# mLSTM output with tokens on the partitions: divisor from two columns of ones beside v

## The chip, the cores and the metric

The kernel runs on one core of a Trainium2 chip, in one launch. The metric is the device time in microseconds (us). Three runs of the kernel before took 1508.81 to 1511.1 us, median 1509.54.

## The reference, cut to what matters

The model is two transformer blocks on 256 tokens of width 1024. The change is in the token mixer of the first block, in the mLSTM (8 heads, 64 wide in q and k, 128 wide in v). The reference walks over chunks of 64 tokens; the kernel computes the same thing for all 256 tokens at once, as masked attention with gate weights. Per head h and token t:

```python
# w[s,t] = (q_t . k_s) * exp(gate terms - m_t), for s <= t, else 0
num[t,:] = sum_s w[s,t] * v[s,:]
den[t]   = sum_s w[s,t]
h[t,:]   = num[t,:] / maximum(abs(den[t]), exp(-m_t))     # exp(-m_t) is "floor" below
hm = h * rsqrt(mean(h*h, axis=-1) + EPS)                  # over the 128 channels of the head
ym = sigmoid(o) * (hm * mh_norm_w)                        # o: one of the projections
```

With D = max(|den|, floor) the division and the norm are one factor: hm = num * rsqrt(sum(num*num)/128 + EPS*D*D). Both kernels use that form, and sigmoid(o) as (1 + tanh(o/2))/2.

## The kernel before, in words

Activations lie with features on the partitions: [128, 8, 256] is 8 tiles of 128 features by 256 tokens. A projection of 128 output features is one `gemm` (L180): 24 matmuls of 256 columns on TensorE, three for each of 8 slices (high half of the weight by high half of the input L185, high by low L186, low by high L187). The weights arrive by DMA (queue of SP, 1 MB each) into three buffers; ScalarE makes the rounded half `wh` (L165) and VectorE or GpSimd the rest `wl` (L166), ahead of the gemm, into a ring of four buffers; a buffer comes free when the gemm that read it is done.

The part around the change, in order:

- L550 to L666: q, k, v and the gates. `wide` makes v with tokens on the partitions, and L209 copies it out of PSUM. `gates` (L612) makes the running sums, the floor (L637, [40, 256], heads on partitions) and the column form `acol` of the gate term (two small transposes, L642, copied at L643).
- L678 `head(h)`: five stages, one taken at each call of `advance`. Scores sc (L681, L682), gate row spread over the partitions (L600), three VectorE operations and an exp for the weights (L686 to L692), the product w (L694), the matmuls num (L697, L698: stationary v, moving w, result features by tokens) and den (L699, L700: stationary `eh(h)`, 40 columns of which two are ones, so that row h of one PSUM tile collects head h), the copy nso (L702), the square sq (L704) and its sum ssq (L705, stationary `eh(h)` again).
- L717: eight rounds of three gemms, with four stages of heads between the gemms of one round, and two slices of the ada projection (L425, VectorE, 32 slices in `adapt`) after each.
- L739: eight gemms for o; the heads left are finished after the first; L747 multiplies nso by 1 + tanh.
- L751 to L759: the factor for all heads as rows [40, 256]: |den|, max with the floor, square, scale, add ssq, root (L757), reciprocal (L758), and its two rounded halves hr.
- L762: eight gemms with tanh (tga). L778: eight more (tgm), and after each one head of `normed` (L769): row h of hr spread over the partitions by a matmul (L600, into the one PSUM tile `bc`), times nso and the norm weight (L773), split into ymh and yml (L262, L263). These feed the branch gemms from about 290 us on.

A planner places all of this: it simulates the engines and orders the instructions of each one by program order among those that are ready. Each engine then takes its own queue strictly in that order and waits where an input is late. All matmuls of `head` have f32 operands, which run as two passes each (the trace counts 16 records for 8 matmuls); those of `gemm` run as one. A transpose on TensorE runs as one.

Of the kernel before, what the change touches and what calls it, by code (L numbers as in the profile page):

```python
# [19 lines left out]
EPS = 1e-6  # L20
# [92 lines left out]
def body(ctx: ExitStack, tc: tile.TileContext, a: dict):  # L113
# [81 lines left out]
    def wide(ws, out, ps_tile, xh, xl, scale=None):  # L195

        ps = [ps_tile() for _ in range(2)]
        for i in range(2):
            wh, wl = next(ws)
            for t in range(2):  # L200
                ts_ = slice(t * 128, (t + 1) * 128)
                for k in range(4):
                    n, kk = slice(256 * k, 256 * k + 256), 4 * i + k
                    T.matmul(ps[t], lhsT=xh[:, kk, ts_], rhs=wh[:, n], start=kk == 0, stop=False)
                    T.matmul(ps[t], lhsT=xl[:, kk, ts_], rhs=wh[:, n], start=False, stop=False)
                    T.matmul(ps[t], lhsT=xh[:, kk, ts_], rhs=wl[:, n], start=False, stop=kk == 7)  # L206
        for t in range(2):
            if scale is None:
                A.copy(out(t), ps[t])  # L209
            else:  # L210
                A.activation(out(t), ps[t], AF.Copy, scale=scale[:, t:t + 1])

# [199 lines left out]
    with ExitStack() as p1:  # L412
# [4 lines left out]
        A.dma_start(out=col, in_=a["cols"])  # L417
        A.dma_start(out=cst["a"], in_=a["ca"])

        def big(name, slot, dt=F32):  # L420
            return f8.tile([128, 8, 256], dt, tag=f"s{slot}", name=name)

        def product(raw, j):
            scr = m1.tile([128, 1024], F32, tag="adas", name="scr", bufs=2)
            return V.scalar_tensor_tensor(out=scr, in0=raw, scalar=0.5, in1=crow, op0=ALU.mult, op1=ALU.mult,  # L425
                                          accum_out=ada[:, j:j + 1])

# [25 lines left out]
        def bct():  # L453
            return bank("bc", 256)
# [5 lines left out]

        def load_c():

            c1, t1 = (m1.tile([128, 1024], F32, tag="adas", name=n, bufs=2)[:1] for n in ("c1", "t1"))
            tc.keep_in_program_order(SY.dma_start(out=c1, in_=a["c"]))
            A.activation(t1, c1, AF.Tanh, scale=0.5)
            V.scalar_tensor_tensor(out=c1, in0=t1, scalar=1.0, in1=c1, op0=ALU.add, op1=ALU.mult)
            for n in range(F0):
                T.matmul(psb[:, :128], lhsT=ones, rhs=ones, start=True, stop=True)
            for i in range(2):
                early[:] = [T.matmul(banks[i], lhsT=ones[:1, :], rhs=c1[:, i * 512:(i + 1) * 512], start=True, stop=True)]  # L470
                A.copy(crow[:, i * 512:(i + 1) * 512], banks[i])
# [14 lines left out]
        def adaload(src, t, n):  # L486
            b = f"{t}{n & 6}"
            if n % 2 == 0:
                if where[b]:
                    stage[b] = f8.tile([128, 2048], F32, tag=f"s{where[b]}", name="araw")  # L490
                else:
                    stage[b] = m1.tile([128, 2048], F32, tag="araw", name="araw", bufs=2)
            raw = halfload(stage[b], src[n // 2], n % 2)
            warm(f"{t}{n}", raw)
            return raw
# [12 lines left out]
        def load_w(n):  # L508
            p = halfload(raws[n // 2], a["wqk"][n // 2], n % 2)
            warm(f"W{n}", p)  # L510
            if n < 4:
                ws.append(split(p, G if WG >> n & 1 else V))
                return
            t = f8.tile([128, 2048], F32R, tag=f"s{(4, 8)[n - 4]}", name="w4")
            with tc.issue_after(made[0].ins), tc.issue_after(made[1].ins):
                A.copy(t[:, :1024], p)
                (G if WG >> n & 1 else V).tensor_sub(t[:, 1024:], p, t[:, :1024].bitcast(F32))
            more.append((t[:, :1024], t[:, 1024:]))
# [72 lines left out]
                V.scalar_tensor_tensor(out=kk[:, j - 4, :], in0=t, scalar=1.0, in1=y, op0=ALU.add, op1=ALU.mult)  # L591

        floor = m1.tile([40, 256], F32, name="floor")
        negm, hr = (m1.tile([40, 256], F32R, name=n) for n in ("negm", "hr"))
        selr = m1.tile([40, 8], F32R, name="selr")

        def spread_row(row, h):
# [8 lines left out]
            A.copy(out, src)  # L606
            V.tensor_sub(out[at:], src[at:n], out[at:].bitcast(F32))

        acol = m1.tile([128, 2, 8], F32, name="acol")
        rw = m1.tile([128, 5, 256], F32, name="rw")  # L610

        def gates(wif):  # L612
# [27 lines left out]
            pt = bct()  # L640
            for t in range(2):
                T.transpose(pt[:, 8 * t:8 * t + 8], g[:8, 3, t * 128:(t + 1) * 128], C("ident")[:8, :8])  # L642
            V.tensor_copy(acol, pt[:, :16].rearrange("p (t h) -> p t h", t=2))  # L643


        v = big("v", 4)
        v4 = v.rearrange("p (t b) n -> p t b n", t=2)
        cv = chunks(a["wv"], range(4), pool_=PV)
        cst["b"] = m1.tile([128, NCST["b"]], F32, name="cb")
        for t in ORD2.split():  # L650
            n = int(t[1])
            if t[0] == "w":
                w67 = split(halfload(raw3, a["wqk"][3], n))
            elif t[0] == "l":
                wif = m1.tile([128, 8, 72], F32, name="wif")
                tc.keep_in_program_order(SY.dma_start(out=wif, in_=a["wif"].rearrange("p (k n) -> p k n", k=8)))
                SY.dma_start(out=cst["b"], in_=a["cb"])
            elif t[0] == "q":
                pss.append(mmt())
                gemm(pss[-1], w67, hh, hl)  # L660
            elif t[0] == "u":
                unit_qk(pss[n], n)
            elif t[0] == "v":
                wide(cv, lambda t: v4[:, t, n, :], mmt, hh, hl)
            elif t[0] == "g":
                gates(wif)  # L666
        vt = v.rearrange("p (t b) n -> p t (b n)", t=2)


        den = bank("den", 256)[:40]  # L670
        ssq = bank("ssq", 256)[:40]

        def eh(h):
            return C("eh")[:, 7 - h:47 - h]

        nso = big("nso", 5)

        def head(h):  # L678
            sc = bank("sc", 384)
# [3 lines left out]
            nb = spread_row(negm, h)  # L683
            yield
            w = m1.tile([128, 384], F32, tag="mw", name="mw", bufs=2)
            V.scalar_tensor_tensor(out=w[:, 0:128], in0=nb[:, 0:128], scalar=acol[:, 0, h:h + 1], in1=C("mneg"),  # L686
                                   op0=ALU.add, op1=ALU.add)
            V.scalar_tensor_tensor(out=w[:, 256:384], in0=nb[:, 128:256], scalar=acol[:, 1, h:h + 1], in1=C("mneg"),
                                   op0=ALU.add, op1=ALU.add)
            V.tensor_scalar(out=w[:, 128:256], in0=nb[:, 128:256], scalar1=acol[:, 0, h:h + 1], scalar2=None,  # L690
                            op0=ALU.add)
            A.activation(w, w, AF.Exp)  # L692
            yield
            V.scalar_tensor_tensor(out=w, in0=sc, scalar=0.03125, in1=w, op0=ALU.mult, op1=ALU.mult)  # L694
            yield
            num = bank("num", 256)
            T.matmul(num, lhsT=vt[:, 0, h * 128:(h + 1) * 128], rhs=w[:, 0:256], start=True, stop=False)  # L697
            T.matmul(num[:, 128:256], lhsT=vt[:, 1, h * 128:(h + 1) * 128], rhs=w[:, 256:384], start=False, stop=True)  # L698
            T.matmul(den, lhsT=eh(h), rhs=w[:, 0:256], start=h == 0, stop=False)  # L699
            T.matmul(den[:, 128:256], lhsT=eh(h), rhs=w[:, 256:384], start=False, stop=h == 7)  # L700
            yield
            A.copy(nso[:, h, :], num)  # L702
            sq = m1.tile([128, 256], F32, tag="sq", name="sq", bufs=4)
            A.activation(sq, num, AF.Square)  # L704
            T.matmul(ssq, lhsT=eh(h), rhs=sq, start=h == 0, stop=h == 7)  # L705
            yield

        def heads():
# [30 lines left out]
        for j, w in enumerate(chunks(a["wo"], range(4))):  # L739
            ps = mmt()  # L740
            gemm(ps, w, hh, hl)
            t = m1.tile([128, 256], F32, tag="cvt", name="cvt", bufs=2)
            A.activation(t, ps, AF.Tanh, scale=0.5)
            advance(bg, 2)
            if j == 0:
                drain(bg)
            V.scalar_tensor_tensor(out=nso[:, j, :], in0=t, scalar=1.0, in1=nso[:, j, :], op0=ALU.add, op1=ALU.mult)  # L747
            advance(bg_ada)


        D2 = rw[:40, 0, :]  # L751
        A.activation(rw[:40, 1, :], den, AF.Abs)
        V.tensor_max(rw[:40, 1, :], rw[:40, 1, :], floor)
        V.tensor_mul(D2, rw[:40, 1, :], rw[:40, 1, :])
        V.tensor_scalar_mul(D2, D2, EPS * 128.0)
        V.tensor_add(D2, D2, ssq)
        A.activation(rw[:40, 2, :], D2, AF.Sqrt, scale=4.0 / 128.0)  # L757
        V.reciprocal(rw[:40, 3, :], rw[:40, 2, :])  # L758
        parts(hr, rw[:40, 3, :], 32)  # L759

        tga, tgm = big("tga", 2), big("tgm", 3)
        for j, w in enumerate(chunks(a["wga"], range(4))):  # L762
# [5 lines left out]

        def normed():  # L769
            for h in range(8):  # L770
                rb = spread_row(hr, h)
                u = m1.tile([128, 256], F32, tag="u", name="u", bufs=2)
                V.scalar_tensor_tensor(out=u, in0=nso[:, h, :], scalar=K("mhw", h), in1=rb, op0=ALU.mult, op1=ALU.mult)  # L773
                split_act(ymh[:, h, :], yml[:, h, :], u)
                yield

        bg = [normed()]
# [760 lines left out]
```

## Time and profile before

| | us |
|---|---|
| median of three runs | 1509.54 |
| the profiled execution, its own time | 1508.95 |
| its span (first to last instruction) | 1507.2 |
| TensorE busy in it | 1453.8 (96%) |
| VectorE busy | 1156.4 (77%) |
| ScalarE busy | 906.3 (60%) |

The heads run from about 100 to 199 us, the gemms of o to 220, tga to 243, `normed` with tgm from 243 to 268. In the chain of waits a line tells the start, the length and the line of a piece; the length is what the instruction adds to the chain, not its own duration. In the table of windows each engine has busy us and instruction count; clock is the granted TensorE clock as a share of 2.4 GHz.

### The profile page before, as it was taken

What the parts mean: (1) busy time and instruction counts of PE and PEld (TensorE: products, weight loads), DVE (VectorE), ACT (ScalarE), POOL (GpSimd) and SP (SyncE); (2) the same over time, 40 slices, a digit from 0 to 9 for tenths busy, and PEclk for the clock granted to TensorE, in tenths of its full rate; (3) what the DMA queues carried; (4) which work ended last, traced back from release to release, by engine and by line L of the source; (5) the groups of instructions that cost most, each with busy time, mean ns of one, the idle gap of its engine ahead of it and who ended that gap; (6) DMA issues with size and microseconds to landing.
All of it is one profiled execution on the core that took longest, in us unless ns stands there. A gap on an engine that the chain in (4) does not pass through costs nothing.

```text
span 1507.2 us, 27126 instructions
## 1 busy us (share of the span) xinstructions
PE 1453.8 (96%) x11020; PEld 1324.7 (88%) x11020; DVE 1156.4 (77%) x2154; ACT 906.3 (60%) x1242; POOL 107.2 (7%) x55
## 2 busy tenths in 40 slices
PE   5899999998998799999999999999999999999998
PEld 4889899997998799999878998777788899899897
DVE  8978797667998927787999887888865679575554
ACT  3554354445543547888877777787755569554543
POOL 3310000004231430000000000000000000000000
PEclk8999999999999999999999999999999999999999
DMA  9556667553434364544455545554555643345542
GB/s 349 182 201 231 229 251 255 181 180 119 169 140 168 112 200 166 169 167 169 144 178 182 169 168 172 183 177 168 168 185 183 219 158 128 104 173 199 180 168 84
DMA packets 40015, 268.63 MB, mean 178 GB/s; under 512 B 4561, under 2 KB 5329, under 8 KB 9170
## 3 DMA queue, kind: packets, MB, share of 16 engines
q1 hardware_dynamic: 38882, 264.67, 50.6%
q10 hardware_dynamic: 1008, 2.23, 0.5%
q8 instruction: 86, 1.41, 0.4%
q14 instruction: 39, 0.32, 0.1%
HBM read 265.83 MB, written 1.05 MB: 177 GB/s over the span
## 4 chain that ended last, share of the span: by engine, by line
PE 83%; DVE 13%; ACT 3%; issue 2%; DMA 0%; DVEq 0%; ACTq 0%
PE mm L185 13%; PE mm L187 13%; PE mm L186 13%; PE acc L255 10%; PE acc L256 10%; PE acc L257 10%; PE g L1069 3%; DVE wl L166 2%; DVE pr L936 1%; PE acc L185 1%; PE acc L187 1%; PE acc L186 1%; DVE scr L425 1%; ACT wh L165 1%; PE mm L206 1%
## 5 line engine op out<-in xcount | busy, mean ns | idle before, releaser
L165 ACT CAST wh<-raw 128x1024 fp32r<-128x1024 f32 x450 | 471.2, 1050 | 472.3 <-PE mm L186 223.9
L166 DVE TENSOR_TENSOR wl<-raw,wh 128x1024 fp32r<-128x1024 f32 x415 | 510.4, 1233 | 181.7 <-ACT wh L165 177.3
L185 PE MATMUL mm<-hh,wh 128*128 128x256 f32 x1816 | 520.4, 287 | 4.6 <-ACT z L871 4.6
L187 PE MATMUL mm<-hh,wl 128*128 128x256 f32 x1816 | 514.9, 284 | 10.2 <-DVE wl L166 10.2
L186 PE MATMUL mm<-hl,wh 128*128 128x256 f32 x1816 | 512.5, 282 | 0.0
L187 PEld LDWEIGHTS mm<-hh,wl 128*128 128x128 f32 x1816 | 345.7, 190 | 12.2 <-DVE wl L166 10.8
L185 PEld LDWEIGHTS mm<-hh,wh 128*128 128x128 f32 x1816 | 344.6, 190 | 11.1 <-ACT z L871 5.2
L186 PEld LDWEIGHTS mm<-hl,wh 128*128 128x128 f32 x1816 | 345.1, 190 | 1.3 <-issue 0.2
L255 PE MATMUL acc<-wh,ah 128*128 128x512 f32 x512 | 205.1, 401 | 1.0 <-ACT ah L262 1.0
L256 PE MATMUL acc<-wh,al 128*128 128x512 f32 x512 | 201.8, 394 | 0.0
L257 PE MATMUL acc<-wl,ah 128*128 128x512 f32 x512 | 201.6, 394 | 0.0
L1047 ACT COPY o<-os 128x1024 f16<-128x1024 f16 x96 | 196.9, 2051 | 1.2 <-DVE os L1044 1.2
L166 POOL TENSOR_TENSOR wl<-raw,wh 128x1024 fp32r<-128x1024 f32 x35 | 90.7, 2596 | 435.7 <-PE mm L326 254.4
L257 PEld LDWEIGHTS acc<-wl,ah 128*128 128x128 f32 x512 | 96.2, 188 | 22.3
L255 PEld LDWEIGHTS acc<-wh,ah 128*128 128x128 f32 x512 | 96.1, 188 | 21.7 <-ACT ah L262 1.1
L256 PEld LDWEIGHTS acc<-wh,al 128*128 128x128 f32 x512 | 96.1, 188 | 20.6
L1072 DVE SCALAR_TENSOR_TENSOR z<-g,z 128x256 f32<-128x256 f32 x128 | 51.1, 419 | 45.5 <-PE g L1069 45.3
L1044 DVE TENSOR_TENSOR os<-io,idxT 128x1024 f16<-128x1024 f16 x96 | 66.2, 689 | 21.8 <-ACT o L1047 21.2
L1054 DVE TENSOR_TENSOR og<-o,gT 128x512 f16<-128x512 f16 (+1 forms) x96 | 82.4, 859 | 0.0
L425 DVE SCALAR_TENSOR_TENSOR scr<-araw,crow 128x1024 f32<-128x1024 f32 x48 | 59.7, 1261 | 2.7 <-DMA araw<-in_wada_dram 2.7
L1069 PEld LDWEIGHTS <-o 128*128 128x128 f16 x1536 | 46.4, 96 | 15.5 <-issue 11.9
L1069 PE MATMUL g<-og,o 128*128 128x32 f16 (+1 forms) x1536 | 56.5, 182 | 0.3 <-ACT o L1047 0.3
(444 smaller groups left out, 1962.6 us busy)
## 6 DMA issues: line engine op xcount, KB each, us to landing
raw<-in_uT_dram SPq DMA_DIRECT2D x64, 1024.0 KB, 4.9
raw<-in_ev_dram SPq DMA_DIRECT2D x64, 1024.0 KB, 4.9
araw<-in_wada_dram SPq DMA_DIRECT2D x16, 1024.0 KB, 6.3
raw<-in_wup_dram SPq DMA_DIRECT2D x16, 1024.0 KB, 4.9
raw<-in_wdn_dram SPq DMA_DIRECT2D x16, 1024.0 KB, 4.9
raw<-in_wcxb_dram SPq DMA_DIRECT2D x12, 1024.0 KB, 4.8
araw<-in_wada_dram SPq DMA_DIRECT2D x16, 512.0 KB, 9.9
raw<-in_wout_dram SPq DMA_DIRECT2D x8, 1024.0 KB, 4.9
```

The lines of the kernel that those rows point to most:

```text
L165: by.copy(wh, raw) if by is A else by.tensor_copy(wh, raw)
L166: on.tensor_sub(wl, raw, wh)
L185: T.matmul(ps, lhsT=wh, rhs=xh, start=start, stop=False, skip_group_check=skip)
L186: T.matmul(ps[:, :n], lhsT=wh, rhs=xl, start=False, stop=False, skip_group_check=skip)
L187: return T.matmul(ps, lhsT=wl, rhs=xh, start=False, stop=stop, skip_group_check=skip)
L255: T.matmul(acc[t][c], lhsT=xh[:, ts_], rhs=wh[:, cs], start=first and n == 0, stop=False)
L256: T.matmul(acc[t][c], lhsT=xl[:, ts_], rhs=wh[:, cs], start=False, stop=False)
L257: T.matmul(acc[t][c], lhsT=xh[:, ts_], rhs=wl[:, cs], start=False, stop=last and n == len(steps) - 1)
L425: return V.scalar_tensor_tensor(out=scr, in0=raw, scalar=0.5, in1=crow, op0=ALU.mult, op1=ALU.mult, accum_out=ada[:, j:j + 1])
L1047: A.copy(o1, os.rearrange("p n t -> p t n"))
L1054: V.tensor_tensor(out=og, in0=o2[:, :, None, :].to_broadcast([128, TB, 2, m]), in1=gT[:, ts_, :, None].to_broadcast([128, TB, 2, m]), op=A ...
L1069: T.matmul(ps[:, t], lhsT=o1[:, t, :], rhs=og[:, t, i], start=i == 0, stop=i == 1)
```

## The change

num is made with tokens on the partitions: w is stationary, v moves, with two columns of ones beside each head's 128 columns, so that column 128 of the result is den for each token. Slots of v are 2080 elements long for this. The floor is transposed too, into `acol`. Per head ScalarE takes |den| of 2 columns, VectorE the maximum and the scaled square, ScalarE the sum of squares along the row (two activations of 128 columns with an accumulator) and the copy of num. tanh(o/2) is kept in a slot of its own (9). The root and reciprocal then work on [128, 16]. In `normed` ScalarE multiplies num by the factor (a scale per partition), TensorE turns each 128x128 tile back, VectorE multiplies by 1 + tanh, and the norm weight goes into the split. To make room, the scratch tile of L425 has one buffer instead of two, and a temporary of the start lies in slot 7.

```diff
 def wide(...):
-                A.copy(out(t), ps[t])
+                o = out(t)
+                A.copy(o, ps[t].rearrange("p (a n) -> p a n", n=o.shape[-1]))
...
+        def slot_of(name, slot, dt=F32):
+            return f8.tile([128, 2080], dt, tag=f"s{slot}", name=name)
...
-            scr = m1.tile([128, 1024], F32, tag="adas", name="scr", bufs=2)
+            scr = m1.tile([128, 1024], F32, tag="adas", name="scr", bufs=1)
...
-        acol = m1.tile([128, 2, 8], F32, name="acol")
+        acol = m1.tile([128, 2, 2, 8], F32, name="acol")
...
                 T.transpose(pt[:, 8 * t:8 * t + 8], g[:8, 3, t * 128:(t + 1) * 128], C("ident")[:8, :8])
-            V.tensor_copy(acol, pt[:, :16].rearrange("p (t h) -> p t h", t=2))
+                T.transpose(pt[:, 16 + 8 * t:24 + 8 * t], floor[:8, t * 128:(t + 1) * 128], C("ident")[:8, :8])
+            V.tensor_copy(acol, pt[:, :32].rearrange("p (i t h) -> p i t h", i=2, t=2))
...
-        v = big("v", 4)
+        v = slot_of("v", 4).rearrange("p (t h n) -> p t h n", t=2, h=8)
+        V.memset(v[:, :, :, 128:130], 1.0)
...
-        nso = big("nso", 5)
+        num_, sto = big("num", 5).rearrange("p (t j) n -> p t (j n)", t=2), big("sto", 9)
+        dv = m1.tile([128, 4, 8, 2], F32, name="dv")
 def head(h):
-            num = bank("num", 256)
-            T.matmul(num, lhsT=vt[:, 0, h * 128:(h + 1) * 128], rhs=w[:, 0:256], start=True, stop=False)
-            T.matmul(num[:, 128:256], lhsT=vt[:, 1, h * 128:(h + 1) * 128], rhs=w[:, 256:384], start=False, stop=True)
-            T.matmul(den, lhsT=eh(h), rhs=w[:, 0:256], start=h == 0, stop=False)
-            T.matmul(den[:, 128:256], lhsT=eh(h), rhs=w[:, 256:384], start=False, stop=h == 7)
+            num = bank("num").rearrange("p (t n) -> p t n", t=2)
+            for t, i in ((0, 0), (1, 0), (1, 1)):
+                T.matmul(num[:, t, :130], lhsT=w[:, (t + i) * 128:(t + i + 1) * 128], rhs=v[:, i, h, :],
+                         start=t == 0, stop=(t, i) != (1, 0), skip_group_check=True)
             yield
-            A.copy(nso[:, h, :], num)
+            d = dv[:, :, h, :]
+            A.activation(d[:, 0, :], num[:, :, 128], AF.Abs)
+            V.tensor_max(d[:, 0, :], d[:, 0, :], acol[:, 1, :, h])
+            V.scalar_tensor_tensor(out=d[:, 0, :], in0=d[:, 0, :], scalar=EPS * 128.0, in1=d[:, 0, :], op0=ALU.mult,
+                                   op1=ALU.mult)
             sq = m1.tile([128, 256], F32, tag="sq", name="sq", bufs=4)
-            A.activation(sq, num, AF.Square)
-            T.matmul(ssq, lhsT=eh(h), rhs=sq, start=h == 0, stop=h == 7)
+            for t in range(2):
+                A.activation(sq[:, :128], num[:, t, :128], AF.Square, accum_out=d[:, 1, t:t + 1])
+            A.copy(num_[:, :, h * 128:(h + 1) * 128], num[:, :, :128])
...
-            t = m1.tile([128, 256], F32, tag="cvt", name="cvt", bufs=2)
-            A.activation(t, ps, AF.Tanh, scale=0.5)
+            A.activation(sto[:, j, :], ps, AF.Tanh, scale=0.5)
...
-            V.scalar_tensor_tensor(out=nso[:, j, :], in0=t, scalar=1.0, in1=nso[:, j, :], op0=ALU.add, op1=ALU.mult)
...
-        D2 = rw[:40, 0, :]
-        A.activation(rw[:40, 1, :], den, AF.Abs)
-        V.tensor_max(rw[:40, 1, :], rw[:40, 1, :], floor)
-        V.tensor_mul(D2, rw[:40, 1, :], rw[:40, 1, :])
-        V.tensor_scalar_mul(D2, D2, EPS * 128.0)
-        V.tensor_add(D2, D2, ssq)
-        A.activation(rw[:40, 2, :], D2, AF.Sqrt, scale=4.0 / 128.0)
-        V.reciprocal(rw[:40, 3, :], rw[:40, 2, :])
-        parts(hr, rw[:40, 3, :], 32)
+        V.tensor_add(dv[:, 2], dv[:, 0], dv[:, 1])
+        A.activation(dv[:, 2], dv[:, 2], AF.Sqrt, scale=4.0 / 128.0)
+        V.reciprocal(dv[:, 3], dv[:, 2])
 def normed():
-                rb = spread_row(hr, h)
+                ps = bct()
+                for t in range(2):
+                    n = num_[:, t, h * 128:(h + 1) * 128]
+                    A.activation(n, n, AF.Copy, scale=dv[:, 3, h, t:t + 1])
+                    T.transpose(ps[:, t * 128:(t + 1) * 128], n, C("ident"))
...
-                V.scalar_tensor_tensor(out=u, in0=nso[:, h, :], scalar=K("mhw", h), in1=rb, op0=ALU.mult, op1=ALU.mult)
-                split_act(ymh[:, h, :], yml[:, h, :], u)
+                V.scalar_tensor_tensor(out=u, in0=sto[:, h, :], scalar=1.0, in1=ps, op0=ALU.add, op1=ALU.mult)
+                split_act(ymh[:, h, :], yml[:, h, :], u, K("mhw", h))
```

## Rows read from the trace of the kernel before

**Rows 1.** The page, chain that ended last: share of the span by engine.

```profile
PE 83%; DVE 13%; ACT 3%; issue 2%; DMA 0%; DVEq 0%; ACTq 0%
```

**Rows 2.** Windows: length, busy us of each engine, PE clock, DMA share, GB/s.

```profile
57.00:100.00 43.00, 36.35 (x272) 34.98 (x271) 35.61 (x60) 21.41 (x37) 9.85 (x4) 0.92 0.56 198
100.00:200.00 100.00, 100.00 (x726) 88.73 (x726) 80.45 (x155) 41.12 (x70) 0.00 (x0) 1.00 0.63 221
200.00:222.00 22.00, 21.97 (x185) 21.77 (x184) 20.98 (x32) 13.82 (x20) 0.00 (x0) 1.00 0.77 275
222.00:243.00 21.00, 21.00 (x178) 20.98 (x177) 17.84 (x34) 8.49 (x14) 0.00 (x0) 1.00 0.95 351
243.00:270.00 27.00, 27.00 (x203) 24.91 (x202) 18.59 (x29) 15.33 (x27) 0.00 (x0) 1.00 0.48 167
```

**Rows 3.** Chain of waits, one head: start, length, line; one of eight.

```profile
122.63 0.43 PE num L697 x2
123.06 0.22 PE num L698 x2
123.28 0.56 PE den L699 x2
123.84 0.22 PE den L700 x2
124.06 0.32 PE mm L185
...
126.85 0.12 PE mm L186
127.09 0.56 PE ssq L705 x2
```

**Rows 4.** Chain of waits, one head of normed; one of eight.

```profile
246.78 0.31 PE bc L600
247.09 0.32 PE mm L185
```

**Rows 5.** Chain of waits, second block: f32 matmuls of 128 columns; transposes of 128x128.

```profile
1290.28 0.22 PE mm L1341 x2
1290.50 0.12 PE acc L185
...
1391.58 0.22 PE pt L1386 x2
1391.79 0.12 PE mm L185
```

**Rows 6.** Chain of waits, the two small transposes of the gates.

```profile
98.09 0.27 PE bc L642 x2
```

**Rows 7.** Waits of VectorE for ScalarE, 100 to 200 us: total, times, longest.

```profile
DVE wl L166 <- ACT wh L165: 4.3, 6, 1.5
...
DVE yal L263 <- ACT yah L262: 0.9, 2, 0.5
DVE negm L607 <- ACT negm L606: 0.5, 1, 0.5
```

**Rows 8.** VectorE groups by shape: busy us, mean ns, idle before.

```profile
L753 DVE TENSOR_TENSOR rw<-rw,floor 40x256 f32<-40x256 f32 x1 | 0.4, 417 | 0.3 <-ACT rw L752 0.3
...
L747 DVE SCALAR_TENSOR_TENSOR nso<-cvt,nso 128x256 f32<-128x256 f32 x8 | 3.3, 415 | 0.0
...
L400 DVE TENSOR_TENSOR sv<-sv 128x4 f32<-128x4 f32 x8 | 1.3, 161 | 0.2
```

**Rows 9.** ScalarE and TensorE groups; the first from 100 to 270 us only.

```profile
L165 ACT CAST wh<-raw 128x1024 fp32r<-128x1024 f32 x48 | 50.2, 1048 | 75.8 <-PE mm L186 49.9 <-issue 18.0 <-DMA raw<-in_wgm_dram 6.4
...
L335 ACT ACTIVATE hh<-x,col 128x256 fp32r<-128x256 f32 x16 | 7.0, 497 | 3.9 <-DVE x L1154 2.3 <-DVE x L1374 1.6
...
L1122 ACT ACTIVATION_READ_ACCUMULATOR yt<-acc 128x1 f32 x4 | 0.8, 198 | 0.0
...
L1386 PE MATMUL pt<-ca,x 128*128 128x128 f32 x16 | 3.0, 272 | 0.0
```

More of the change, by code (lines that the diff above doesn't have):

```diff
@@ L418, in body @@
         A.dma_start(out=cst["a"], in_=a["ca"])
+        def slot_of(name, slot, dt=F32):
+            return f8.tile([128, 2080], dt, tag=f"s{slot}", name=name)
         def big(name, slot, dt=F32):
-            return f8.tile([128, 8, 256], dt, tag=f"s{slot}", name=name)
+            return slot_of(name, slot, dt)[:, :2048].rearrange("p (j n) -> p j n", j=8)
         def product(raw, j):
-            scr = m1.tile([128, 1024], F32, tag="adas", name="scr", bufs=2)
+            scr = m1.tile([128, 1024], F32, tag="adas", name="scr", bufs=1)
             return V.scalar_tensor_tensor(out=scr, in0=raw, scalar=0.5, in1=crow, op0=ALU.mult, op1=ALU.mult,
@@ L461, in load_c @@
         def load_c():
-            c1, t1 = (m1.tile([128, 1024], F32, tag="adas", name=n, bufs=2)[:1] for n in ("c1", "t1"))
+            c1, t1 = m1.tile([128, 1024], F32, tag="adas", name="c1", bufs=1)[:1], slot_of("t1", 7)[:1, :1024]
             tc.keep_in_program_order(SY.dma_start(out=c1, in_=a["c"]))
@@ L489, in adaload @@
                 if where[b]:
-                    stage[b] = f8.tile([128, 2048], F32, tag=f"s{where[b]}", name="araw")
+                    stage[b] = slot_of("araw", where[b])[:, :2048]
                 else:
@@ L513, in load_w @@
                 return
-            t = f8.tile([128, 2048], F32R, tag=f"s{(4, 8)[n - 4]}", name="w4")
+            t = slot_of("w4", (4, 8)[n - 4], F32R)[:, :2048]
             with tc.issue_after(made[0].ins), tc.issue_after(made[1].ins):
@@ L593, in body @@
         floor = m1.tile([40, 256], F32, name="floor")
-        negm, hr = (m1.tile([40, 256], F32R, name=n) for n in ("negm", "hr"))
+        negm = m1.tile([40, 256], F32R, name="negm")
         selr = m1.tile([40, 8], F32R, name="selr")
@@ L642, in gates @@
                 T.transpose(pt[:, 8 * t:8 * t + 8], g[:8, 3, t * 128:(t + 1) * 128], C("ident")[:8, :8])
-            V.tensor_copy(acol, pt[:, :16].rearrange("p (t h) -> p t h", t=2))
-        v = big("v", 4)
-        v4 = v.rearrange("p (t b) n -> p t b n", t=2)
+                T.transpose(pt[:, 16 + 8 * t:24 + 8 * t], floor[:8, t * 128:(t + 1) * 128], C("ident")[:8, :8])
+            V.tensor_copy(acol, pt[:, :32].rearrange("p (i t h) -> p i t h", i=2, t=2))
+        v = slot_of("v", 4).rearrange("p (t h n) -> p t h n", t=2, h=8)
+        V.memset(v[:, :, :, 128:130], 1.0)
         cv = chunks(a["wv"], range(4), pool_=PV)
@@ L663, in body @@
             elif t[0] == "v":
-                wide(cv, lambda t: v4[:, t, n, :], mmt, hh, hl)
+                wide(cv, lambda t: v[:, t, 2 * n:2 * n + 2, :128], mmt, hh, hl)
             elif t[0] == "g":
                 gates(wif)
[L667 to L674, printed above, removed]
-        nso = big("nso", 5)
+        num_, sto = big("num", 5).rearrange("p (t j) n -> p t (j n)", t=2), big("sto", 9)
+        dv = m1.tile([128, 4, 8, 2], F32, name="dv")
         def head(h):
@@ L685, in head @@
             w = m1.tile([128, 384], F32, tag="mw", name="mw", bufs=2)
-            V.scalar_tensor_tensor(out=w[:, 0:128], in0=nb[:, 0:128], scalar=acol[:, 0, h:h + 1], in1=C("mneg"),
+            V.scalar_tensor_tensor(out=w[:, 0:128], in0=nb[:, 0:128], scalar=acol[:, 0, 0, h:h + 1], in1=C("mneg"),
                                    op0=ALU.add, op1=ALU.add)
-            V.scalar_tensor_tensor(out=w[:, 256:384], in0=nb[:, 128:256], scalar=acol[:, 1, h:h + 1], in1=C("mneg"),
+            V.scalar_tensor_tensor(out=w[:, 256:384], in0=nb[:, 128:256], scalar=acol[:, 0, 1, h:h + 1], in1=C("mneg"),
                                    op0=ALU.add, op1=ALU.add)
-            V.tensor_scalar(out=w[:, 128:256], in0=nb[:, 128:256], scalar1=acol[:, 0, h:h + 1], scalar2=None,
+            V.tensor_scalar(out=w[:, 128:256], in0=nb[:, 128:256], scalar1=acol[:, 0, 0, h:h + 1], scalar2=None,
                             op0=ALU.add)
```

## The prediction, made before the changed kernel was run

> **What bounds the kernel now.** I read the chain of waits first: 83% of it is TensorE [rows 1]. Then the windows, to see whether that holds where the change is: from 100 to 270 us TensorE is busy for 169.97 of 170 us at the full clock (1.00 granted, the 2.4 GHz level) [rows 2]. In that stretch every microsecond that TensorE no longer needs is a microsecond of the kernel, as long as nothing else takes over. The next candidate stands in the same rows: VectorE is busy for 80.45 of 100 us in the heads, and 20.98 of 22 us right behind them. ScalarE is at 41 of 100, and the DMA queue has its peak only later (0.95 in 222 to 243 us). Before 100 us it is different: TensorE has 36.35 of 43 us there, so latencies through VectorE count. Last I read the chain again, head by head, for prices: a length there is what an instruction adds to TensorE's row, which is what a sum needs; the durations of the groups overlap.
>
> **What goes from TensorE, per head.** num costs 0.43 + 0.22, den 0.56 + 0.22, and the first gemm matmul behind them has 0.32 instead of the ordinary 0.12 [rows 3]. The 0.13 that L699 takes more than L697 for the same 256 columns, and the 0.20 behind, come with the stationary operand of 40 columns: f32 matmuls with a full 128x128 one are followed by a plain 0.12 [rows 5]. So num and den: 0.43 + 0.22 + 0.56 + 0.22 + 0.20 = 1.63 us. ssq: 0.56 [rows 3] and the same 0.20 behind it, 0.76. The spread of hr: 0.31, and 0.32 behind it instead of 0.12 [rows 4], 0.51. Together 2.90 us a head, 8 heads: 23.2 us.
>
> **What comes to TensorE.** Three f32 matmuls of 130 columns with a full stationary operand. The nearest row is one of 128 columns at 0.22 [rows 5], so 3 x 0.22 x 130/128 = 0.67. From below, nothing for the two columns: 0.66. From above, if the narrow end brought the 0.20 of den along: 0.87. I take 0.67, since shape and type are those of the row but for two columns. Two transposes of 128x128 cost 0.22 together in the chain [rows 5]. From above, the small transposes of the gates: 0.27 for two and 0.20 behind [rows 6], 0.47. I take 0.22, the row of the same shape, between the same kind of matmuls. Together 0.89 a head, 7.1 us for eight. The two new transposes of the floor are of the small kind: 0.47 once. TensorE's sum is 23.2 - 7.1 - 0.5 = 15.6 us less; with both upper bounds it is 15.6 - 8 x (0.20 + 0.25) = 12.0.
>
> For the transposes the trace shows a duration of 272 ns each [rows 9], but only 0.11 each in the chain, because the next instruction starts inside it. The Trainium skill, TensorE: Matmul & The Clock Gate, Part 4, puts one in a kernel at about 275 ns, calls access latency the larger part of it, and says the full clock doesn't engage for them. The duration agrees; by the rule as a price the sum would be 2.6 us smaller, by the chain it is not.
>
> **VectorE in the heads.** It gains two operations of 2 columns per head; the nearest are those of 128x4 at 0.16 [rows 8], so 8 x 2 x 0.16 = 2.6 us. It loses four operations of the L753 kind (at most 4 x 0.42 = 1.7) and one L747 (0.42) [rows 8]. 80.45 + 2.6 - 2.1 = 81.0. TensorE's 100 us shrink there by 8 x (1.63 + 0.76 - 0.67) = 13.8, to 86.2. Of VectorE's 19.55 idle us, those spent waiting for TensorE shrink with it, but 4.3 + 0.9 + 0.5 = 5.7 were waits for ScalarE [rows 7]. 81.0 + 5.7 = 86.7, and the new maximum waits for ScalarE's absolute value: at 0.2 a head 1.6 more, 88.3. So VectorE needs 2.1 us more than TensorE offers: I take a loss of 2. Its bounds are 0 (the stretch from 200 to 222 us runs at 95% VectorE without stopping TensorE [rows 2]; the weight ring is four deep) and 13.8 (all 19.55 idle us stay).
>
> **What lies beside other work.** ScalarE per head: absolute value about 0.2, two squares and two accumulator reads of 0.198 [rows 9] where one square was. About 0.9 a head, 7 us on 41 of 86: hidden; if ScalarE were late, num's one PSUM tile would hold the next head, but heads are some 15 us apart. In `normed`, scaling a tile of 128 columns is estimated at 0.39 (0.497 for 256 columns with a scale per partition [rows 9], less about 0.11 for half the columns), twice, and 0.1 more in the split. ScalarE had 15.33 of 27 us [rows 2]; 8 x 0.88 = 7 more makes 22 of some 25. The copies of v only get a stride: nothing. The memset of the ones waits for the last matmul that reads slot 4; it is tiny, and the planner puts it where that is done. If it stood too early, the q and k work behind it on VectorE would wait, before 100 us, where such a wait counts; I give that region 0, with -2 to +2 for a new order. The small operations on [128, 16] replace L753 to L758 and seven L747: VectorE gets 5 us free from 200 us on, where TensorE is full anyway, so nothing. The single scratch buffer is written by VectorE alone, in its own order: nothing. The slot 7 temporary is dead long before its next load: nothing. No DMA is added; SP's loads follow buffers that come free sooner, at 221 GB/s in the heads with room to the 351 seen [rows 2]. Behind 270 us all is as before, only earlier.
>
> **The sum.** 15.6 - 2 = 13.6 us off the profiled execution: 1508.95 - 13.6 = 1495.4. The median of the runs lies 0.59 above that execution, so 1495.9; I say 1496.
>
> **Rivals.** (a) *The turn back is dearer.* TensorE takes its queue in order, and each transpose waits for a scaling by ScalarE, which also has the weight copies of 1.05 us [rows 9] in its row. If each head's transposes meet one such copy: 8 x 1.05 = 8.4 us given back, 1504. At the durations instead of the chain's lengths (8 x 2 x (0.27 - 0.11) = 2.6): 1498.5; that is what the page's rule on transposes would give. Against both: ScalarE idles 75.8 us ahead of those copies [rows 9], so the scalings have room ahead of need.
> (b) *VectorE holds the heads.* If its idle time stays, the 13.8 go, and the gain is 15.6 - 13.8 = 1.8: 1507.7. For it: 81.0 of 86.2 is 94%. Against: most of the idle time is waiting for TensorE.
> (c) *Slower: the maximum waits behind weight copies.* ScalarE stands idle before 30 of its copies until TensorE frees a ring buffer (49.9 us, 1.66 each [rows 9]), in order. If the absolute value of each head is queued behind such a copy, VectorE stops at the maximum for 1.66 + 1.05 = 2.7 us, and with it the next `wl`. 8 x 2.7 = 21.7, VectorE needs 81.0 + 5.7 + 21.7 = 108.4 where the stretch had 100: 8.4 longer, less the 2.3 of `normed`, plus 0.5: 6.6 slower, 1516. It decides from 1.9 us a head. For it: this part of ScalarE's row is mostly such waits. Against: today the copy nso and the square stand in that same place, and VectorE's waits for ScalarE are 5.7 us in all [rows 7].
> (d) *Full gain*, no loss in VectorE: 1493.9.
>
> **Chances.** Forecast with (d), 1491 to 1498: 0.58. (a), 1498 to 1505: 0.22. (b), 1505 to 1509: 0.13. (c): 0.07. A measurement of this kernel tells about 0.2%, 3 us, from no change. Faster by more, below 1506.5: 0.58 + 0.22 + 0.06 = 0.86. Within: 0.07. Slower: 0.07. The range 1491 to 1504 leaves out (b), (c) and little else.
>
> **What would show it.** In the profile after: no den and ssq lines; three num lines of about 0.22 in the chain, with 0.12 behind them; two transposes at 0.22 in place of 0.51; the heads 12 to 14 us shorter with TensorE still full. TensorE waiting for VectorE's `wl` in the heads would show (b), for a scaling in `normed` (a), VectorE waiting for the absolute value by more than 1 us a head (c). A changed stretch before 100 us would make the forecast wrong by something that I priced at nothing.

## The result, and the profile after

The changed kernel takes 1493.36 us (median of 4 runs, 1492.74 to 1494.06) against 1509.17 for the kernel before in the same session: 15.8 us less, ratio 0.9895, 95% interval 0.9880 to 0.9911. Its profiled execution took 1493.74, 15.2 less than that of before. Page of the changed kernel, span and chain that ended last:

```profile
span 1491.9 us, 27112 instructions
...
PE 81%; DVE 12%; ACT 3%; DMA 2%; issue 1%; SPq 0%; DVEq 0%; ACTq 0%
```

Windows of the changed kernel, columns as in [rows 2]; the heads, the gemms of o, tga, and tgm with `normed`:

```profile
103.00:186.00 83.00, 83.00 (x669) 80.60 (x668) 75.17 (x157) 41.52 (x92) 0.00 (x0) 1.00 0.68 241
186.00:207.00 21.00, 21.00 (x180) 21.00 (x179) 19.32 (x31) 17.16 (x39) 0.00 (x0) 1.00 0.89 339
207.00:228.00 21.00, 21.00 (x180) 21.00 (x179) 19.04 (x35) 9.40 (x14) 0.00 (x0) 1.00 0.98 357
228.00:255.00 27.00, 27.00 (x231) 27.00 (x230) 17.42 (x25) 15.94 (x28) 0.00 (x0) 1.00 0.55 191
```

TensorE is still full in all four, so what it lost is what the kernel gained. In the chain of the changed kernel one head's num is now a single piece, and the next matmul of a gemm follows at its ordinary 0.12, where [rows 3] had 0.32:

```profile
122.52 0.12 PE mm L187
122.64 0.67 PE num L698 x6
123.30 0.12 PE mm L185
```

Six records are three f32 matmuls of two records each: 0.22 a matmul. In the same chain the two transposes of a head of `normed` stand where [rows 4] had 0.31 and 0.32:

```profile
231.00 0.22 PE bc L771 x2
231.22 0.12 PE mm L185
```

Marks along the way say where the 15.3 us of span came from. Each is a first start in the view by tile: the gates' first operation on VectorE, the first spread of the gate row, the first tanh of tgm, and the first sum behind the branch gemms.

| stretch | before | after | difference |
|---|---|---|---|
| start to gates | 91.1 | 91.6 | +0.5 |
| gates to first head | 10.5 | 11.6 | +1.1 |
| first head to first tgm | 143.3 | 128.7 | -14.6 |
| first tgm to branches | 48.2 | 46.3 | -1.9 |
| branches to the end | 1214.1 | 1213.7 | -0.4 |

The first stretch is nothing of the change: in eleven profiled executions of these kernels the gates begin anywhere from 90.2 to 92.1 us. Edits of a few microseconds are therefore read below from their own stretch. The 1.1 in the second belongs to the change; the run with the floor late, below, takes it back. Chain of the changed kernel at the gates (an `issue` piece is time for which the profile shows no wait):

```profile
100.60 0.42 ACT floor L642
101.02 0.04 issue
101.07 0.22 PE bc L648
101.29 0.06 PE bc L647
101.35 0.06 PE bc L648
101.41 0.32 PE mm L186
```

And TensorE's waits from 57 to 300 us, the one row that before had not:

```profile
PE bc L648 <- ACT floor L642: 0.7, 1, 0.7
```

The planner put the first transpose of the floor (L648) into TensorE's queue ahead of its input, and TensorE stood 0.7 us for ScalarE, in front of the second transpose of the gate term (L647). VectorE copies both with one instruction, so the gate term, which was long ready, also came late.

### The profile page after: what moved, and what is told of

Read it like the earlier page. It is cut to its first block, busy times and chain, and to the rows that moved or that the text cites. A ratio compares the mean times of both kernels' runs of the same rounds, so it can differ in the third digit from the quotient of the medians.

```text
span 1491.9 us, 27112 instructions
## 1 busy us (share of the span) xinstructions
PE 1435.5 (96%) x10998; PEld 1318.5 (88%) x10998; DVE 1151.9 (77%) x2159; ACT 913.7 (61%) x1288; POOL 106.0 (7%) x55
## 4 chain that ended last, share of the span: by engine, by line
PE 81%; DVE 12%; ACT 3%; DMA 2%; issue 1%; SPq 0%; DVEq 0%; ACTq 0%
PE mm L185 13%; PE mm L187 13%; PE mm L186 13%; PE acc L256 10%; PE acc L257 10%; PE acc L258 10%; PE g L1069 3%; DVE wl L166 2%; DMA araw<-in_wada_dram 2%; DVE pr L936 1%; PE acc L185 1%; PE acc L187 1%; PE acc L186 1%; ACT wh L165 1%; DVE scr L429 1%
## 5 line engine op out<-in xcount | busy, mean ns | idle before, releaser
L187 PEld LDWEIGHTS mm<-hh,wl 128*128 128x128 f32 x1816 | 345.2, 190 | 11.6 <-DVE wl L166 11.4
L1069 PEld LDWEIGHTS <-o 128*128 128x128 f16 x1536 | 46.4, 96 | 15.6 <-issue 11.9
```

The costliest lines, as they stand in the source:

```text
L187: return T.matmul(ps, lhsT=wl, rhs=xh, start=False, stop=stop, skip_group_check=skip)
L1069: T.matmul(ps[:, t], lhsT=o1[:, t, :], rhs=og[:, t, i], start=i == 0, stop=i == 1)
```

## The experiments

The theory: TensorE's row sets the end from the gates to 330 us, and each instruction costs there what the chain charges for it, the 0.20 behind a narrow operand included. Rivals: the gain is VectorE's relief or a lucky order of the queues; the lengths belong to the moving columns; a transpose costs its duration; VectorE was about to take over. All kernels but "before, wide operand" are edits of the changed kernel. The stretches in this table are the third and fourth of the one above. Their marks can fall a few matmuls of a gemm (0.12 each) earlier or later from run to run, so where it matters the two are read together.

| run | median, us | first head to tgm | tgm to branches |
|---|---|---|---|
| before | 1508.7 to 1509.2 | 143.3 | 48.2 |
| changed kernel | 1493.36 | 128.7 | 46.3 |
| den put back | 1501.08 | 136.6 | 46.3 |
| spread put back | 1498.39 | 128.7 | 50.0 |
| before, wide operand | 1505.42 | 138.1 | 48.8 |
| turn twice | 1496.01 | 128.7 | 48.1 |
| floor late | 1492.76 | 128.9 | 46.3 |
| spread on 128 partitions | 1490.19 | 126.0 | 46.3 |
| both of these | 1490.05 | 126.2 | 46.3 |
| one more VectorE operation a head | 1493.81 | 128.6 | 47.2 |
| three more | 1511.88 | 145.0 | 47.2 |

**den put back.**

```diff
...
+            T.matmul(den, lhsT=eh(h), rhs=w[:, 0:256], start=h == 0, stop=False)
+            T.matmul(den[:, 128:256], lhsT=eh(h), rhs=w[:, 256:384], start=False, stop=h == 7)
```

> The changed kernel, with den's two matmuls (stationary operand of 40 columns) put back behind num, their result unread. Price list (TensorE's chain sets the end, every length returns): 8 x (0.56 + 0.22 + 0.20) = 7.8 us, so 1493.4 + 7.8 = 1501.2. If the gain came from somewhere else (VectorE freed, another order of the queues) and TensorE has slack in the heads: within 2 us of 1493.4. By the count of columns alone, without the cost of the narrow operand: 8 x 0.65 = 5.2, 1498.6.

Measured 7.7 us more than the changed kernel, 7.9 in the heads. The price list holds; slack or a lucky order would have hidden it. Its chain, one head:

```profile
108.62 0.67 PE num L703 x6
109.29 0.56 PE den L705 x2
109.85 0.22 PE den L706 x2
110.06 0.31 PE mm L185
```

**Spread put back.**

```diff
+                T.matmul(bank("ssq", 256), lhsT=selr[:, h:h + 1].to_broadcast([40, 128]), rhs=negm, start=True, stop=True)
```

> The changed kernel, with one spread of a row (40x256, stationary 40x128, as hr had it) put back ahead of each head's turn, its result unread. Price list: 8 x 0.51 = 4.1 us, 1497.5. By the count of columns alone (one pass of 256 columns, 0.12): 8 x 0.12 = 1.0, 1494.4. If the stretch of normed is not bound by TensorE: 1493.4.

The stretch grew by 3.7 us, the median by 5.0 (its four runs scatter over 3.8). In the chain a spread costs 0.31, and the transposes right behind it take the cost of the switch, 0.37 instead of 0.22. That is 0.46 a head and 3.7 for eight, near the 0.51 of the price list and not the 0.12 of its columns:

```profile
233.13 0.31 PE ssq L767
233.44 0.37 PE bc L772 x2
```

**The kernel before, den and ssq with a wide operand.**

```diff
-("eh", 47)
+("eh", 135)
...
-            return C("eh")[:, 7 - h:47 - h]
+            return C("eh")[:, 7 - h:135 - h]
...
```

> The kernel before, with the stationary operand of den and ssq 128 columns wide instead of 40 (95 more columns of zeros in the constant, rows 40 to 127 of the result unread); matmuls and moving columns stay the same. If the narrow operand itself costs (0.13 in the instruction and 0.20 behind it, once for den and once for ssq): 8 x 0.66 = 5.3 us faster than before, 1503.9. If the lengths belong to the moving columns: 1509.2, no change.

The heads are 5.2 us shorter with the same matmuls and moving columns. Chain of this kernel, one head, to be read against [rows 3]:

```profile
122.31 0.43 PE num L697 x2
122.75 0.22 PE num L698 x2
122.97 0.43 PE den L699 x2
123.40 0.22 PE den L700 x2
123.62 0.12 PE mm L185
...
126.46 0.43 PE ssq L705 x2
126.89 0.12 PE mm L185
```

The 0.13 and the 0.20 are gone: they were the narrow operand's. The median moved by 3.3 (ratio 0.9975, interval 0.9963 to 0.9986, which is 2.1 to 5.6 us). In the profiled execution, the slowest of the seven (1508.67), the stretch behind the branches, which the edit doesn't touch, was 4 us longer than before. Most of it was lost where the trace of before stands at 473 to 492 us, far from the edit; why is open.

**Turn twice.**

```diff
-                    T.transpose(ps[:, t * 128:(t + 1) * 128], n, C("ident"))
+                    for _ in range(2):
+                        T.transpose(ps[:, t * 128:(t + 1) * 128], n, C("ident"))
```

> The changed kernel, with each of the 16 transposes of normed issued twice to the same place. By the chain's length (0.11 each): 16 x 0.11 = 1.8 us, 1495.2. By the duration (0.272 each, and about 275 ns in the Trainium skill, TensorE: Matmul & The Clock Gate, Part 4): 4.4 us, 1497.8. If they run beside other work: 1493.4.

1.8 us in the stretch, the chain's price (the median moved 2.7, its runs scatter over 3.3). Chain of this kernel, four transposes:

```profile
229.58 0.44 PE bc L772 x4
230.02 0.12 PE mm L185
```

**Floor late.**

```diff
-                T.transpose(pt[:, 16 + 8 * t:24 + 8 * t], floor[:8, t * 128:(t + 1) * 128], C("ident")[:8, :8])
...
+            if h == 0:
+                pt = bank("den", 256)
+                for t in range(2):
+                    T.transpose(pt[:, 8 * t:8 * t + 8], floor[:8, t * 128:(t + 1) * 128], C("ident")[:8, :8])
+                V.tensor_copy(acol[:, 1], pt[:, :16].rearrange("p (t h) -> p t h", t=2))
```

> The changed kernel, with the two small transposes of the floor taken out of the gates step and put into head 0, ahead of its num, in another PSUM bank, with a copy of their own. In the changed kernel TensorE stood 0.75 us for the floor, and one transpose of the gate term was queued behind it. If that wait is on the path: 0.8 to 1.2 us faster than the changed kernel, 1492.4. If VectorE's latency there sets the pace anyway: 1493.4.

Gates to first head: 10.5 us again, 1.1 less; 0.2 comes back in the heads, where the two transposes now stand. TensorE's wait for the floor is gone. The median moved 0.6, which the scatter of the runs alone could give; the stretch shows the effect.

**Spread on 128 partitions.**

```diff
-        negm = m1.tile([40, 256], F32R, name="negm")
-        selr = m1.tile([40, 8], F32R, name="selr")
+        negm = m1.tile([128, 256], F32R, name="negm")
+        selr = m1.tile([128, 8], F32R, name="selr")
+        A.activation(negm, ones[:, 0:1].to_broadcast([128, 256]), AF.Copy, scale=0.0)
...
-            T.matmul(ps, lhsT=selr[:, h:h + 1].to_broadcast([40, 128]), rhs=row, start=True, stop=True)
+            T.matmul(ps, lhsT=selr[:, h:h + 1].to_broadcast([128, 128]), rhs=row, start=True, stop=True)
...
```

> The changed kernel, with the gate row's spread (8 matmuls) on 128 partitions instead of 40: the selector and the row are filled up with zeros, same 256 moving columns. If the operand of 40 rows itself costs (0.31 in the instruction and 0.20 behind it, where a full one takes 0.12): 8 x 0.39 = 3.1 us faster than the changed kernel, 1490.3. If the length belongs to something else (the wait for the row, the switch between kinds of operands): 1493.4.

2.7 us less from the first head on, 3.0 from the gates on (the mark of the first head moved by 0.3), 3.2 in the median. The same matmul with 88 more partitions of zeros costs less; chain of this kernel:

```profile
116.12 0.22 PE sc L682 x2
116.34 0.12 PE bc L605
116.46 0.12 PE mm L185
```

**Both.** The two edits in one kernel.

> The two edits together: the floor's transposes late, and the gate row's spread on 128 partitions. If both are on TensorE's path they add: 4 us faster than the changed kernel, 1489.3. If VectorE takes over in the heads (it had 76.8 of 86 us): no better than the better one alone, about 1490.3.

1490.05, ratio to before 0.9878 (0.9861 to 0.9894). It beats both kernels, the changed one by some 3 us. From the gates to the first tgm the late floor alone saved 0.9 us, the wide spread alone 3.0, both together 3.6, so in the trace they nearly add. The medians don't show it: 1490.05 can't be told from the 1490.19 of the spread alone, and it is what the rival gave. But the rival's cause is not there: in these heads TensorE was busy for 83.00 of 83 us and VectorE for 77.63.

**One more VectorE operation per head, then three (the second line in a loop of three).**

```diff
+            idle = m1.tile([128, 1024], F32, tag="adas", name="idle", bufs=1)
+            V.scalar_tensor_tensor(out=idle, in0=crow, scalar=0.5, in1=crow, op0=ALU.mult, op1=ALU.mult)
```

> The changed kernel, with one more VectorE operation of 128x1024 (about 1.15 us) per head behind the three that make the weights, its result unread; 9.2 us of VectorE work in the heads, where it stood idle for 9.2 of 86 us. By the sum of the prediction (VectorE needs 88.3 of 86.2 already): 9 us slower than the changed kernel, 1502.5. If the ring of weights and the later, emptier stretch take up what is late: under 3 us slower, below 1496.4.

> The changed kernel, with three more VectorE operations of 128x1024 per head, their results unread: 24 x 1.15 = 27.6 us. In the run with one more, VectorE was busy for 79.9 of 83 us of the heads and TensorE lost nothing. If VectorE's busy time alone is the limit (TensorE loses only what does not fit): the changed kernel has 75.2 of 83 there, 20 us too many, and the 150 us to the end of normed have some 21 idle, 6.6 us too many: between 7 and 20 us slower, 1500 to 1513. If the ring of weights takes up even this: within 3 us of 1493.4.

One more cost 0.4 us in the median, and 0.8 from the first head to the branches (the planner put seven of the eight in the heads, one at 47 us). Three more cost 18.5. Windows of the heads in both, columns as above, and of the gemms of o with three:

```profile
103.00:186.00 83.00, 82.92 (x663) 80.12 (x662) 79.93 (x162) 41.37 (x92) 0.00 (x0) 1.00 0.68 239
```

```profile
103.00:202.00 99.00, 87.22 (x670) 82.86 (x669) 95.66 (x178) 43.37 (x98) 0.00 (x0) 0.98 0.57 201
202.00:224.00 22.00, 22.00 (x174) 22.00 (x175) 21.14 (x35) 12.29 (x23) 0.00 (x0) 0.93 0.93 342
```

VectorE at 96% left TensorE full, but with nothing to spare. In the kernel with one more, the chain runs over ScalarE and VectorE from 172.83 us on and comes back to TensorE through a `wl` that is a little late:

```profile
184.58 1.14 DVE wl L166
185.72 0.04 issue
185.77 0.39 PE mm L187
```

So the seven operations in the heads (8.5 us, 1.217 each) are about what VectorE had to spare, near its 7.8 idle us of 83. At 97% of a longer stretch it set the pace, and TensorE stood for 11.8 of 99 us (waits from 100 to 275 us of the kernel with three):

```profile
PE mm L187 <- DVE wl L166: 6.4, 4, 2.1
PE num L701 <- DVE mw L696: 3.1, 3, 2.3
```

The 18.5 lie near the 20 that the expectation gave for the heads alone, far from the 6.6 with the later stretch counted in. They are no clean price of VectorE's work: behind these stands the granted clock fell too, to a mean of 0.93 from 202 to 224 us, where the gemms of o of the changed kernel had 1.00.

## Why the prediction was right, and where it was not

- *TensorE's sum.* 15.6 us by lengths from the chain, with the cost behind narrow operands in it. The third stretch gave 14.6 where the terms for it make 14.1 (8 x 1.72 and the first head's 0.29); the fourth gave 1.9 of the 2.0 left for seven heads. Put back one by one, den and the spread returned near what was priced for them. ssq was not put back: of the 16.5 us of both stretches, den (7.9), the spread against the turn (8 x 0.29) and num leave 6.5 for it, where 8 x 0.76 = 6.1 were priced. The 0.4 too much is not accounted for.
- *The two added columns and the transposes.* 0.67 and 0.22 as priced. The duration of a transpose is 272 ns here too, and the granted clock was 1.00 all through `normed` [above, 228 to 255 us]. The figure in the Trainium skill, TensorE: Matmul & The Clock Gate, Part 4, about 275 ns (the page speaks of bf16), fits the duration of these f32 ones, but not the cost between other matmuls, and its remark on the clock doesn't show here, where transposes stand among gemms.
- *The gates.* Priced at 0.5 as two small transposes; 1.1 measured. The wait of TensorE for the floor was missing: what mattered was where the planner queues the transposes and what stands behind them.
- *The step that was mis-sized: a loss of 2 in VectorE.* TensorE stayed full, and the time came out near rival (d), 1493.9, and 2.6 us under the 1496; the range held because it had (d) in it. Two things made the term too big. From 103 to 189 us, the stretch that was to hold 81.0 us of VectorE's work, it was busy for 77.4:

```profile
103.00:189.00 86.00, 86.00 (x695) 83.60 (x694) 77.44 (x163) 42.43 (x99) 0.00 (x0) 1.00 0.69 246
```

And I counted 5.7 us of waits for ScalarE as fixed and added 1.6 of new ones. They were slack, not work, and shrank when the stretch got tight. VectorE's waits for ScalarE in the heads of the changed kernel come to 3.2 us:

```profile
DVE wl L166 <- ACT wh L165: 2.4, 3, 1.2
...
DVE yal L264 <- ACT yah L263: 0.4, 1, 0.4
DVE dv L704 <- ACT dv L703: 0.4, 1, 0.4
```

- *Rival (b)* was real, but some 8 us of VectorE work away. *Rival (c)* did not come: the maximum waited 0.4 us for the absolute value in this stretch, and 1.1 us in all eight heads. *Rival (a)* did not come either. The planner ran all 16 scalings early, from 195.5 to 202.4 us, while the first transposes start at 230.8; view by tile of the changed kernel (duration min/median/max, first and last start):

```profile
L770 ACT ACTIVATE num<-num,dv x16: 396/403/419, 195.5 to 202.4; 128x128 f32<-128x128 f32 x16
...
L771 PE MATMUL bc<-ca,num x16: 270/272/276, 230.8 to 252.4; 128*128 128x128 f32 x16
```

- *What I priced at nothing* before 100 us stayed at nothing beyond the gates.

## What to carry to other kernels

Where one engine is full and the chain runs along it, price an edit by the lengths in the chain, the longer piece behind an instruction included, and not by durations. Idle time of the next engine made of waits is a reserve: count its work alone against the new stretch. After moving an input's producer, look at what the planner queues behind its consumer.

## What the runs showed that was not expected

A stationary operand of 40 columns, or of 40 partitions, cost time by itself between gemms of full ones. With 40 columns, an f32 matmul of 256 columns took 0.56 instead of 0.43 and the next full one 0.32 instead of 0.12; with 40 partitions, a single-pass one took 0.31 instead of 0.12, with the same behind it. The second of two narrow ones in a row took no more than a full one (L700 in [rows 3], 0.22), so the extra stands where full and narrow change over. Filling up with zeros made eight spreads some 3 us cheaper, and den and ssq of the kernel before 5.2.
